# A hybrid retention and sparse-attention block: the first weighing one tile later, index pairs and selection steps at other places, the first attention scores in written order

## The chip, the cores and the metric

The kernel runs on one core of a Trainium2 chip. The metric is the device time of one execution in microseconds (us). The engines that matter here are TensorE (PE, matrix products into PSUM), VectorE (DVE), ScalarE (ACT), GpSimd (POOL) and the queue that issues most transfers (SP). Each engine works through its own list of instructions in order and waits on semaphores for the others.

## The reference

One block of a model of width 1024 over 16 meta tokens and 512 real ones, in float32: a gated feed-forward part, a mixer, a second feed-forward part and a last norm. The mixer multiplies its normalised input by one wide matrix and cuts the product into the operands of two branches:

```python
proj = u @ w_in
rq, rk, rv, rg, aq, ak, av, iq, ik, iw, g_ret, g_att = jnp.split(proj, offs, axis=-1)
# retention: 4 heads, keys of 256, values of 512, decay by distance; then a norm per head
yr = (jax.nn.silu(rg) * retention(rope(rq), rope(rk) * RET_DK**-0.5, rv)) @ w_ret_out
# sparse attention: 8 heads of 128; index scores choose the 128 keys of each query
score = einsum('bqh,bqhs->bqs', wi, relu(einsum('bqhd,bsd->bqhs', qi, ki))) * idx_scale
_, sel = lax.top_k(score, k_top)          # among admissible keys; meta keys always count
p = softmax(scores of the selected and the meta keys)
ya = (p @ v) @ w_att_out
merged = sigmoid(g_ret) * yr + sigmoid(g_att) * ya
return merged @ w_mix_out
```

## The kernel before

Every float32 product is made of three: each operand is split into a high part (a copy on ACT, `split` and `in_two`, L282 or L117) and a low part (the difference on DVE, L283 or L118), and PE adds high x high, high x low and low x high in PSUM (`mm3`, L157). A weight tile is fetched into `raw` (two buffers), split into `whi` and `wlo` (three buffers each), and used for one output tile of 128 rows; the 1024 of the inner dimension are eight steps k of three matmuls. `between` lets a projection do other work ahead of a chosen k: an entry `(4, pair)` runs `pair` ahead of k = 4.

PSUM has a ring of four one-bank tiles (`sm_tile`) and one of two two-bank tiles (`mm_tile`) in the mixer. A new tile takes the place of the fourth (second) last one and so waits for the last reader of that.

The order on PE is written by hand everywhere. In the retention part the orders on ACT and DVE are too: a list of steps, one for each weight tile, is walked by `steps_through`, which fetches and splits two tiles ahead and calls each step's matmuls and what stands behind them. For each retention head h the list has `queries_keys(h)` (two tiles of rq, two of rk), `gates_of(h)` (four tiles of rg) and `outputs(h - 1)` (four steps of two psro tiles, each added into `accr` by DVE, L1691, and behind the last the five psst tiles of the decayed score matrix of the next head, L1439 to L1443). While the projections of head h run, head h - 1 is finished: `weigh(p, c)` multiplies values by the score matrix into pspv (13 matmuls, L1460 and L1461), takes the product with the gate (`to`, L1471) and the square; `norm_sums` and `norm_all` sum the squares over all columns on PE (psn) with a diagonal matrix that `norm_diag` splits in between.

The index branch runs beside it. Its queries and keys are rotated and split (`index_queries`, `index_keys`), and `pair` takes one step of `index_steps`: two index heads for one block of 128 queries, six matmuls into two pssc tiles (L1250), a relu on ACT (L1253) and a weighted sum on DVE. There are twelve such steps; the first also transposes the index weights (psw, L1239). `pick` takes one step of `select_steps`: the next eight largest of a row and their replacement by a marker (L1267 and L1268), sixteen times for each of three blocks of 512, 384 and 256 columns; after a block's last pick, `bias` (L1270) is written. What is left of it after the last output is done beside the start of the attention.

The attention part multiplies, for each of eight heads, queries and keys into psS and psS3 (`scores`, L1864), adds the bias and takes the row maximum on DVE (L1867, L1869), the exponential on ACT (L1870) and the division on DVE (L1872, L1873); then come the projections of the next head's q and k (psaq, psak), the transposition of the probabilities (`transpose_p`, psPT, L1880) with their split, one projection of a gate (`wide_gate`), and the product with the values (psao, again `weighted`, L1460 and L1461). In this part only PE's order is written; the other engines' is made by the scheduler, except for a short stretch at the start, which stands under `manual_schedule(engines=BUSY)` and ends with the gates 4 and 5 (`gate_acc`, on POOL, L1320).

Of the kernel before, what the change touches and what calls it, by code (L numbers as in the profile page):

```python
# [18 lines left out]
P = 128  # L19
# [3 lines left out]
NM = 16  # L23
# [58 lines left out]
def kernel(ctx: ExitStack, tc: tile.TileContext, x, meta, g1, wg1, wu1, wd1, gm,  # L82
# [1247 lines left out]
    if True:  # L1330
# [207 lines left out]
        def pick(n):  # L1538

            for _ in range(n):  # L1540
                next(picks["steps"], None)
# [23 lines left out]
        def gates_of(h):  # L1565

            p = h - 1

            def behind_0(ps):
                silu(h, ps)  # L1570
                if h:
                    low = norm_diag(p)
                    if h > 1:
                        pick(1)
                    low()

            def behind_1(ps):
                silu(h, ps)
                if h == 0:
                    decayed(0)  # L1580
                    index_queries(0)
                else:
                    two_normed_parts(p, 0)

            def behind_2(ps):
                silu(h, ps)
                if h == 0:
                    index_queries(1)
                    index_queries(2)
                else:  # L1590
                    two_normed_parts(p, 2)

            def behind_3(ps):
                silu(h, ps)
                if h == 0:
                    index_queries(3)
                    values_in(0)
                    picks["pairs"] = index_steps()
                    picks["steps"] = select_steps()
                elif h == 1:  # L1600
                    for _ in picks["pairs"]:
                        pass
                else:
                    if h == RH - 1:
                        weigh(h, 0)
                    pick(3)

            sums, spread = (6, lambda: norm_sums(p)), (4, lambda: norm_all(p))
            inside = [()] * 4
            if h == 1:  # L1610
                inside = [((1, pair), (4, pair), sums), ((1, pair), spread, (6, pair)), ((1, pair), (4, pair), (6, pair)),
                          ((1, pair), (3, pair), (6, pair))]
            elif h:
                some_picks = (3, lambda: pick(1))
                inside = [(sums,), (spread,), (some_picks,), (some_picks,)]
            runs = [proj("psrg", REAL, i, b) for i, b in zip(inside, (behind_0, behind_1, behind_2, behind_3))]
            if h == 0:
                run0 = runs[0]

                def first(w, lower):  # L1620
                    bring_index()
                    run0(w, lower)

                runs[0] = first
            return steps_of(tiles(("rg", h), w_in, OFF_RG + h * DV, 4), runs)

        def queries_keys(h):

            pss, p = {}, h - 1
            ropes = heads[h]["ropes"] = {}  # L1630

            def q0(ps):
                pss["qa"] = ps
                if h == 1:
                    index_keys(0)
                    index_keys(1)
                weigh(p, 0)
                if h == 1:
                    index_keys(2)

            def q1(ps):
                pss["qb"] = ps
                ropes["q"] = rope_pieces(pss["qa"], ps, cos[:, REAL], sin[:, REAL], S, ret_q)
                some(ropes["q"], 5)
                weigh(p, 1)

            def k0(ps):
                pss["ka"] = ps
                some(ropes["q"], 1)
                weigh(p, 2)  # L1650
                some(ropes["q"], 1)

            def k1(ps):
                ropes["k"] = rope_pieces(pss["ka"], ps, cos, sin, T, ret_k)
                weigh(p, 3)

            inside = ((3, pair), (6, pair)) if h == 1 else ()
            return (steps_of(tiles(("rq", h), w_in, OFF_RQ + h * DK, 2), [proj("psrq", REAL, (), q0), proj("psrq", REAL, (), q1)])
                    + steps_of(tiles(("rk", h), w_in, OFF_RK + h * DK, 2), [proj("psrk", None, (), k0), proj("psrk", None, inside, k1)]))

        def outputs(h, beside):

# [36 lines left out]
        def beside_outputs(h):  # L1699
            def beside(i):  # L1700
                if i < 3:
                    some(heads[h + 1]["ropes"]["k"], (3, 3, 1)[i])
                pick(2 if h == 0 and i == 2 else 1)
            return beside

        last_gates, first_kq = [], []
# [17 lines left out]

        def last_2(ps):
            first_kq.append(ps)
            low = norm_diag(p)
            pick(1)
            low()

        def last_3(ps):
            first_kq.append(ps)
# [77 lines left out]
    with pool("ao") as ao:  # L1810
        vo = [ao.tile([P, AH, S], F32R, tag=f"vo{i}", name="vo") for i in range(2)]
        ao_parts = [(vo[0][:, c, :], vo[1][:, c, :]) for c in range(AH)]
        with pool("at") as at:
# [11 lines left out]
            cq, ck = (Cols(w_in, o_ + P, AH - 1, step=1) for o_ in (OFF_AQ, OFF_AK))  # L1825
            scale = DH**-0.5

            def proj_q():
                w = cq.next()
                ps = sm_tile("psaq")  # L1830
                mm3([(ps, REAL)], w, xs, KD)
                return rope_q(ps)
# [13 lines left out]
            def rope_k(ps, eng=nc.gpsimd):  # L1846
# [2 lines left out]
                split(y, k[0], k[1])  # L1849
                return k  # L1850

            def scores(q, k):
                for j in (2, 1, 0, 3):
                    n = NM + P * (j + 1)
                    qs = slice(j * P, (j + 1) * P)
                    if j < 3:
                        ps = sm_tile("psS")
                        outs = [(ps[:, : max(n, 256)], slice(0, max(n, 256)))]
                        sv = ps[:, :n]
                    else:  # L1860
                        outs, sv = halves(mm_tile("psS3"))
                    for i, (a, b) in enumerate(((q[0], k[0]), (q[0], k[1]), (q[1], k[0]))):
                        for o_, sl in outs:
                            nc.tensor.matmul(o_, a[:, qs], b[:, sl], start=i == 0, stop=i == 2)  # L1864
                    s = tmp()
                    m = at.tile([P, 4], F32, tag="stat", name="stat", bufs=8)
                    nc.vector.tensor_tensor_reduce(s[:, :n], sv, bias[j], 1.0, MARK, ALU.add,  # L1867
                                                   ALU.max, m[:, 0:1])
                    nc.vector.tensor_scalar(m[:, 1:2], m[:, 0:1], -scale, None, ALU.mult)  # L1869
                    nc.scalar.activation(prob[j][:, :n], s[:, :n], AF.Exp, bias=m[:, 1:2], scale=scale,  # L1870
                                         accum_out=m[:, 2:3])
                    nc.vector.reciprocal(m[:, 3:4], m[:, 2:3])  # L1872
                    nc.vector.tensor_scalar(prob[j][:, :n], prob[j][:, :n], m[:, 3:4], None, ALU.mult)  # L1873

            def transpose_p():
                parts = []
                for kb in range(4):
                    ps = sm_tile("psPT")
                    for j in range(max(kb - 1, 0), 4):
                        nc.tensor.transpose(ps[:, j * P : (j + 1) * P], prob[j][:, kb * P : (kb + 1) * P], ident)  # L1880
                    if kb == 3:
                        nc.tensor.transpose(ps[:NM, 0:P], prob[3][:, 4 * P : T], ident)
                    n = S - KQ[kb]
                    ph = at.tile([P, wide(n)], F32R, tag=f"pth{kb}", name="pth")[:, :n]
                    pl = at.tile([P, wide(n)], F32R, tag=f"ptl{kb}", name="ptl")[:, :n]
                    split(ps[:, KQ[kb] :], ph, pl)
                    parts.append((ph, pl))
                split_rows(ps[:NM, P - NM : P], tp["p"][:, :NM], "hlh")
                return parts

            def weigh_v(h, parts, v):
# [12 lines left out]
            with tc.manual_schedule(engines=BUSY):  # L1904
                w = gr.next()
                k, q = rope_k(first_k, nc.vector), rope_q(first_q, nc.vector)
                t, t5 = (at.tile([P, S], F32, tag="gate", name="gate", bufs=2) for _ in range(2))
                nc.scalar.activation(t, first_gate, AF.Sigmoid)
                gate_acc(4, t)
                ps = mm_tile("psgate")[:, :S]  # L1910
                mm3([(ps, REAL)], w, xs, KD)
                nc.scalar.activation(t5, ps, AF.Sigmoid)
                gate_acc(5, t5)
            for h in range(AH):
                more = h + 1 < AH
                scores(q, k)
                if h == 0:
                    vs = split_values(raw, [v[:, :4, :] for v in vo])
                    raw = fetch_values(5, vraw())
                if more:  # L1920
                    q, k = proj_q(), proj_k()
                else:
                    wide_gate()
                    wide_gate()
# [291 lines left out]
```

## Time and profile before

| | |
|---|---|
| median of 3 runs | 1543.66 us (1541.44 to 1543.89) |
| profiled execution | 1541.07 us, span 1539.3 us |
| PE busy | 1518.3 us, 99% of the span |
| DVE busy | 1092.5 us, 71% |
| ACT busy | 727.2 us, 47% |
| POOL busy | 105.7 us, 7% |
| granted clock of PE, mean | 0.997 |

The profile shows one execution. Rows of a timeline give the start on the axis of the span, the duration, the engine, the line, the operation, output <- inputs, shapes and, in brackets, how long the engine had been idle and what ended that. Buffer numbers are left out of the names, so all tiles of one name are alike.

### The profile page before, as it was taken

What the parts mean: (1) busy time and instruction counts of PE and PEld (TensorE: products, weight loads), DVE (VectorE), ACT (ScalarE), POOL (GpSimd) and SP (SyncE); (2) the same over time, 40 slices, a digit from 0 to 9 for tenths busy, and PEclk for the clock granted to TensorE, in tenths of its full rate; (3) what the DMA queues carried; (4) which work ended last, traced back from release to release, by engine and by line L of the source; (5) the groups of instructions that cost most, each with busy time, mean ns of one, the idle gap of its engine ahead of it and who ended that gap; (6) DMA issues with size and microseconds to landing.
All of it is one profiled execution on the core that took longest, in us unless ns stands there. A gap on an engine that the chain in (4) does not pass through costs nothing.

```text
span 1539.3 us, 23919 instructions
## 1 busy us (share of the span) xinstructions
PE 1518.3 (99%) x9779; PEld 1368.7 (89%) x9779; DVE 1092.5 (71%) x1672; ACT 727.2 (47%) x1138; POOL 105.7 (7%) x133
## 2 busy tenths in 40 slices
PE   9999999999999999999999999999999999999997
PEld 8999999999888887688888878998888899899996
DVE  4998585776877757676958797666455788586675
ACT  5655353554354444443333346667335356254453
POOL 1000000002111120000000122111002000000000
PEclk9999999999999999999999999999999999999999
DMA  5132333226453462232313242223343223333232
GB/s 167 60 125 90 111 102 103 98 97 218 165 197 135 141 194 91 85 127 78 117 61 99 94 126 74 83 81 116 125 149 103 97 78 101 110 103 117 83 119 87
DMA packets 150701, 173.48 MB, mean 113 GB/s; under 512 B 4928, under 2 KB 122200, under 8 KB 149952
## 3 DMA queue, kind: packets, MB, share of 16 engines
q1 hardware_dynamic: 141952, 151.58, 30.4%
q0 software_dynamic: 3808, 11.38, 1.9%
q10 hardware_dynamic: 4832, 9.00, 1.7%
q8 instruction: 76, 1.25, 0.3%
q14 instruction: 33, 0.27, 0.0%
HBM read 155.94 MB, written 16.01 MB: 112 GB/s over the span
## 4 chain that ended last, share of the span: by engine, by line
PE 85%; issue 10%; DVE 2%; ACT 1%; POOL 1%; DMA 1%; SPq 0%; ACTq 0%; POOLq 0%; DVEq 0%
PE psqX L157 14%; PE psd L157 8%; PE psd L2070 7%; PE psqY L157 7%; PE psvX L1118 4%; PE psro L157 4%; PE psqZ L157 3%; PE psak L157 3%; PE psu L157 3%; PE psga L157 3%; PE psmo L157 3%; PE psat L157 3%; PE psaq L157 3%; PE psg L157 2%; PE psgate L157 2%
## 5 line engine op out<-in xcount | busy, mean ns | idle before, releaser
L283 DVE TENSOR_TENSOR wlo<-raw,whi 128x1024 fp32r<-128x1024 f32 (+2 forms) x184 | 198.9, 1084 | 49.1 <-ACT whi L282 49.0
L282 ACT ACTIVATE whi<-raw 128x1024 fp32r<-128x1024 f32 (+2 forms) x184 | 169.8, 924 | 124.3 <-PE psd L157 37.3
L157 PE MATMUL psqX<-tl,whi 128*128 128x264 f32 (+1 forms) x432 | 122.3, 283 | 0.0
L157 PE MATMUL psqX<-th,whi 128*128 128x264 f32 (+1 forms) x432 | 122.3, 283 | 0.0
L157 PE MATMUL psqX<-th,wlo 128*128 128x264 f32 (+1 forms) x432 | 122.2, 283 | 0.0
L118 DVE TENSOR_TENSOR wlo<-raw,whi 128x1024 fp32r<-128x1024 f32 (+1 forms) x60 | 73.0, 1217 | 53.9 <-ACT whi L117 52.9
L282 ACT ACTIVATE whi<-wsum 128x1024 fp32r<-128x1024 f32 x72 | 76.3, 1060 | 70.7 <-PE psd L2070 22.0
L117 ACT ACTIVATE whi<-raw 128x1024 fp32r<-128x1024 f32 (+1 forms) x60 | 62.6, 1044 | 97.5 <-PE psat L157 26.6
L283 DVE TENSOR_TENSOR wlo<-wsum,whi 128x1024 fp32r<-128x1024 f32 x72 | 87.9, 1221 | 12.5 <-ACT whi L282 12.5
L157 PEld LDWEIGHTS psqX<-th,whi 128*128 128x128 f32 x432 | 82.1, 190 | 0.1
L157 PEld LDWEIGHTS psqX<-th,wlo 128*128 128x128 f32 x432 | 82.0, 190 | 0.0
L157 PEld LDWEIGHTS psqX<-tl,whi 128*128 128x128 f32 x432 | 82.0, 190 | 0.0
L157 PE MATMUL psro<-vo,whi 128*128 128x512 f32 x256 | 80.3, 394 | 0.5 <-DVE vo L283 0.5
L157 PE MATMUL psd<-hl,whi 128*128 128x264 f32 x352 | 71.3, 284 | 0.0
L157 PE MATMUL psd<-hh,wlo 128*128 128x264 f32 x352 | 70.7, 283 | 0.0
L157 PE MATMUL psd<-hh,whi 128*128 128x264 f32 x352 | 70.7, 282 | 0.0
L2070 PE MATMUL psd<-whi,hh 128*128 128x512 f32 x176 | 68.5, 389 | 0.0
L2070 PE MATMUL psd<-wlo,hh 128*128 128x512 f32 x176 | 68.5, 389 | 0.0
L2070 PE MATMUL psd<-whi,hl 128*128 128x512 f32 x176 | 68.5, 389 | 0.0
L157 PEld LDWEIGHTS psro<-vo,whi 128*128 128x128 f32 x256 | 48.1, 188 | 11.9 <-DVE vo L283 1.1
L157 PEld LDWEIGHTS psd<-hh,wlo 128*128 128x128 f32 x352 | 54.4, 188 | 0.0
L157 PEld LDWEIGHTS psd<-hh,whi 128*128 128x128 f32 x352 | 54.1, 188 | 0.0
(445 smaller groups left out, 4521.9 us busy)
## 6 DMA issues: line engine op xcount, KB each, us to landing
raw<-in_ffn_w_up_dram SPq DMA_DIRECT2D x22, 1024.0 KB, 5.0
raw<-in_ffn_w_gate_dram SPq DMA_DIRECT2D x21, 1024.0 KB, 5.0
raw<-in_w_in_dram SPq DMA_DIRECT2D x19, 1024.0 KB, 5.0
raw<-in_w_in_dram SPq DMA_DIRECT2D x31, 512.0 KB, 3.5
raw<-in_ffn_w_down_dram SPq DMA_DIRECT2D x24, 512.0 KB, 3.5
w<-in_w_in_dram SPq DMA_DIRECT2D x24, 512.0 KB, 6.3
raw<-in_ffn_w_down_dram SPq DMA_DIRECT2D x12, 768.0 KB, 4.3
raw<-in_w_ret_out_dram SPq DMA_DIRECT2D x8, 1024.0 KB, 4.8
```

Source lines behind the costliest of these rows:

```text
L117: nc.scalar.activation(hi, src, AF.Copy)
L118: eng.tensor_tensor(lo, src, hi.bitcast(F32), ALU.subtract)
L157: nc.tensor.matmul(o, a[:, k, :], b[:, sl], start=first and k == 0 and i == 0, stop=last and k == nk - 1 and i == 2, skip_group_check=onto)
L282: nc.scalar.activation(hi, src, AF.Copy)
L283: return lambda: nc.vector.tensor_tensor(lo, src, hi.bitcast(F32), ALU.subtract)
L1118: nc.tensor.matmul(d[bank_][t], a, b[:, k, :], start=not onto and j + k + m == 0, stop=j + k == 3 and m == 2, skip_group_check=onto)
L2070: nc.tensor.matmul(ps, a[:, bs], m[:, j, :], start=first and i == 0, stop=last and i == 2)
```

## The change

- For h = 1 the weighing of the first value tile, and with it all that hangs on it (13 matmuls, the product, the square), comes behind the second rq tile in place of the first; the three `index_keys` come together behind the first.
- The twelve index pairs get other places: one ahead of k = 5 in the first rk tile, and others in the four rg tiles.
- `norm_diag` makes its low part at once, ahead of a pick.
- More picks stand in the tiles of h = 2 and 3 and in the last two steps of `outputs(0)` to `outputs(2)`, so that all 48 and the three bias steps are done by the last output step.
- The four scores of the first attention head are written out with the two divisions of each behind all four, under the written order on PE, ACT and DVE; the next q weight is taken ahead of them. In `transpose_p` the tail rows are split ahead of the last block.

The count of instructions is the same.

```diff
@@ gates_of(h)
             def behind_0(ps):
                 silu(h, ps)
                 if h:
-                    low = norm_diag(p)
+                    norm_diag(p)()
                     if h > 1:
                         pick(1)
-                    low()
...
             if h == 1:
-                inside = [((1, pair), (4, pair), sums), ((1, pair), spread, (6, pair)), ((1, pair), (4, pair), (6, pair)),
-                          ((1, pair), (3, pair), (6, pair))]
+                inside = [((2, pair), (4, pair), sums), ((1, pair), spread, (6, pair)), ((4, pair), (6, pair)),
+                          ((3, pair), (5, pair), (7, pair))]
             elif h:
-                some_picks = (3, lambda: pick(1))
-                inside = [(sums,), (spread,), (some_picks,), (some_picks,)]
+                one_pick = (3, lambda: pick(1))
+                inside = [(sums,), (spread, (6, lambda: pick(1))), (one_pick,), (one_pick,)]
@@ queries_keys(h)
             def q0(ps):
                 pss["qa"] = ps
                 if h == 1:
-                    index_keys(0)
-                    index_keys(1)
-                weigh(p, 0)
-                if h == 1:
-                    index_keys(2)
+                    for i in range(3):
+                        index_keys(i)
+                else:
+                    weigh(p, 0)
+                    pick(1)
 
             def q1(ps):
                 pss["qb"] = ps
                 ropes["q"] = rope_pieces(pss["qa"], ps, cos[:, REAL], sin[:, REAL], S, ret_q)
+                if h == 1:
+                    weigh(p, 0)
                 some(ropes["q"], 5)
                 weigh(p, 1)
 
...
                 weigh(p, 2)
                 some(ropes["q"], 1)
+                if h > 1:
+                    pick(1)
 
             def k1(ps):
                 ropes["k"] = rope_pieces(pss["ka"], ps, cos, sin, T, ret_k)
                 weigh(p, 3)
-
-            inside = ((3, pair), (6, pair)) if h == 1 else ()
+                if h > 1:
+                    pick(1)
+
+            inside = [((5, pair),), ((3, pair), (6, pair))] if h == 1 else [(), ()]
@@ beside_outputs(h)
-                pick(2 if h == 0 and i == 2 else 1)
+                pick(2 if i > 1 else 1)
@@ last_2(ps)
-            low = norm_diag(p)
+            norm_diag(p)()
             pick(1)
-            low()
@@ attention
-            def proj_q():
-                w = cq.next()
+            def proj_q(w=None):
+                w = w or cq.next()
...
+            def score(j, q, k):
+                n = NM + P * (j + 1)
...
+                def to_one():
+                    nc.vector.reciprocal(m[:, 3:4], m[:, 2:3])
+                    nc.vector.tensor_scalar(prob[j][:, :n], prob[j][:, :n], m[:, 3:4], None, ALU.mult)
+
+                return to_one
+
             def scores(q, k):
                 for j in (2, 1, 0, 3):
...
+                    score(j, q, k)()
...
+                    if kb == 3:
+                        split_rows(ps[:NM, P - NM : P], tp["p"][:, :NM], "hlh")
                     split(ps[:, KQ[kb] :], ph, pl)
                     parts.append((ph, pl))
-                split_rows(ps[:NM, P - NM : P], tp["p"][:, :NM], "hlh")
...
                 gate_acc(5, t5)
+                w = cq.next()
+                for to_one in [score(j, q, k) for j in (2, 1, 0, 3)]:
+                    to_one()
             for h in range(AH):
                 more = h + 1 < AH
-                scores(q, k)
-                if h == 0:
+                if h:
+                    scores(q, k)
+                else:
                     vs = split_values(raw, [v[:, :4, :] for v in vo])
                     raw = fetch_values(5, vraw())
                 if more:
-                    q, k = proj_q(), proj_k()
+                    q, k = proj_q(w if h == 0 else None), proj_k()
```

More of the change, by code (lines that the diff above doesn't have):

```diff
@@ L1655, in k1 @@
                 weigh(p, 3)
-            inside = ((3, pair), (6, pair)) if h == 1 else ()
+                if h > 1:
+                    pick(1)
+            inside = [((5, pair),), ((3, pair), (6, pair))] if h == 1 else [(), ()]
             return (steps_of(tiles(("rq", h), w_in, OFF_RQ + h * DK, 2), [proj("psrq", REAL, (), q0), proj("psrq", REAL, (), q1)])
-                    + steps_of(tiles(("rk", h), w_in, OFF_RK + h * DK, 2), [proj("psrk", None, (), k0), proj("psrk", None, inside, k1)]))
+                    + steps_of(tiles(("rk", h), w_in, OFF_RK + h * DK, 2), [proj("psrk", None, inside[0], k0), proj("psrk", None, inside[1], k1)]))
         def outputs(h, beside):
@@ L1850, in rope_k @@
                 return k
+            def score(j, q, k):
+                n = NM + P * (j + 1)
+                qs = slice(j * P, (j + 1) * P)
+                if j < 3:
+                    ps = sm_tile("psS")
+                    outs = [(ps[:, : max(n, 256)], slice(0, max(n, 256)))]
+                    sv = ps[:, :n]
+                else:
+                    outs, sv = halves(mm_tile("psS3"))
+                for i, (a, b) in enumerate(((q[0], k[0]), (q[0], k[1]), (q[1], k[0]))):
+                    for o_, sl in outs:
+                        nc.tensor.matmul(o_, a[:, qs], b[:, sl], start=i == 0, stop=i == 2)
+                s = tmp()
+                m = at.tile([P, 4], F32, tag="stat", name="stat", bufs=8)
+                nc.vector.tensor_tensor_reduce(s[:, :n], sv, bias[j], 1.0, MARK, ALU.add,
+                                               ALU.max, m[:, 0:1])
+                nc.vector.tensor_scalar(m[:, 1:2], m[:, 0:1], -scale, None, ALU.mult)
+                nc.scalar.activation(prob[j][:, :n], s[:, :n], AF.Exp, bias=m[:, 1:2], scale=scale,
+                                     accum_out=m[:, 2:3])
+                def to_one():
+                    nc.vector.reciprocal(m[:, 3:4], m[:, 2:3])
+                    nc.vector.tensor_scalar(prob[j][:, :n], prob[j][:, :n], m[:, 3:4], None, ALU.mult)
+                return to_one
@@ L1852, in scores @@
             def scores(q, k):
                 for j in (2, 1, 0, 3):
[L1854 to L1871, printed above, removed]
@@ L1872, in scores @@
-                    nc.vector.reciprocal(m[:, 3:4], m[:, 2:3])
-                    nc.vector.tensor_scalar(prob[j][:, :n], prob[j][:, :n], m[:, 3:4], None, ALU.mult)
+                    score(j, q, k)()
             def transpose_p():
@@ L1913 @@
                 gate_acc(5, t5)
+                w = cq.next()
+                for to_one in [score(j, q, k) for j in (2, 1, 0, 3)]:
+                    to_one()
             for h in range(AH):
                 more = h + 1 < AH
-                scores(q, k)
-                if h == 0:
+                if h:
+                    scores(q, k)
+                else:
                     vs = split_values(raw, [v[:, :4, :] for v in vo])
```

## The prediction, made before the change was run

> **What bounds the kernel now.** I read the table of engines first, then the list of everything that TensorE (PE) waited for in the whole run.
>
> ```profile
> PE 1518.3 (99%) x9779; PEld 1368.7 (89%) x9779; DVE 1092.5 (71%) x1672; ACT 727.2 (47%) x1138; POOL 105.7 (7%) x133
> PE pspv L1460 <- ACT vo L282: 2.9, 1, 2.9
> PE psS L1864 <- ACT aq L117: 2.0, 1, 2.0
> PE psS L1864 <- DVE aq L118: 1.9, 1, 1.9
> PE pssc L1250 <- ACT tmp L1253: 1.7, 2, 1.1
> ...
> PE psn L1506 <- DVE tmp L283: 1.1, 2, 0.6
> PE psao L1461 <- issue: 0.9, 1, 0.9
> PE psro L157 <- DVE vo L283: 0.5, 2, 0.2
> ```
>
> The first row gives busy us, share and instruction count; the others what PE waited for: us in total, times, longest. PE is busy 99% and the change neither adds nor removes a matmul, so all it can win is idle time of PE. The waits that it touches sum to 2.9 + 2.0 + 1.9 + 1.7 + 1.1 + 0.9 = 10.5 us, plus matmuls that run slowly after such a wait. Everything else it does is move VectorE (DVE) work under PE's matmuls or out from under them. Times below are on the axis of this execution, 1541.07 us (its span of 1539.3 and 1.8 around it); the median of the runs is 1543.66, so I add 2.6 at the end. A measurement of this kernel can tell about 0.2%, 3.1 us, from no change.
>
> **First weighing one tile later (h = 1).** The first pspv waits for the highs of the values. The timeline there (start, duration, and in brackets the idle time before it and what ended it), and PE in the stretches of the first and the second pspv (length, busy us, granted clock, DMA share, GB/s):
>
> ```profile
> 590.02 0.50 PE L1460 MATMUL pspv<-ph,vo 128*128 128x512 f32 x1 [2.85 <-ACT vo L282]
> 590.02:592.40 2.38, 2.38 (x14) 1.00 0.83 289
> 597.97:599.98 2.01, 2.01 (x15) 1.00 0.00 0
> 586.36 1.23 DVE L283 TENSOR_TENSOR wlo<-raw,whi 128x1024 fp32r<-128x1024 f32 x1 [2.50 <-ACT whi L282]
> ...
> 590.00 2.50 DVE L283 TENSOR_TENSOR vo<-vraw,vo 128x512 fp32r<-128x512 f32 x4 [0.74 <-ACT vo L282]
> ...
> 596.35 1.41 DVE L1379 TENSOR_TENSOR ikl<-tmp,ikh 64x512 fp32r<-64x512 f32 x2
> ...
> 602.25 0.68 DVE L1402 TENSOR_TENSOR tmp<-psrq,sin 128x512 f32<-128x512 f32 x1
> 610.18 0.35 PE L1239 MATMUL psw<-ident,iw 8*128 8x8 f32 x3
> 610.46 0.50 PE L1250 MATMUL pssc<-ikh,iqh 64*128 64x512 f32 x2
> ```
>
> After the change the second rq tile starts at 587.0 in place of that wait. Its third matmul needs the weight lows that end at 587.59, so 0.2 is lost at once; the projection takes 5.6, the value parts are long done at 592.5, and both weighings and the first rk tile follow without a wait. That is 2.85 - 0.2 won, and 0.4 more because the waiting pspv took 2.38 for the matmuls that the next one does in 2.01, at a granted clock of 1.00 in both: about 3.0. [...]
>
> Then it is given back. A pair of index scores and the small transposes psw now stand inside the first rk tile, at k = 5, about 3.65 after that tile's start at 596.6, so at 600.3. They take PSUM tiles of a ring of four, whose last users are the first pspv (its square on ACT, ready about 600.5) and the two psrq tiles, read last by the fourth and fifth rope piece. DVE's queue there is unchanged but that one product `to` (0.68) goes behind the rk weight lows: index-key lows end at 597.76, weight lows 599.3, `to` 599.9, then five rope pieces at a pitch of 0.6, the last ending at about 603.0 (before: 602.25 + 0.68 = 602.9). Without a wait the second score matmul would start at 600.9, so PE stands 2.1 there. What is queued behind it is the rest of the rk tile; nobody else is held. So: 3.0 - 2.1 = 0.9 won. The bounds: nothing lost, if those tiles come free earlier than I read, and 3.0, if the rope pieces slip by another weight's lows.
>
> **Index pairs at other places.** There are twelve pairs before and after. The two waits of pssc (1.7 in all; they are at k = 1 of the last two rg tiles, where a pair follows the previous one too closely) lose their cause: no pair stands at k = 1 there now. -1.7; the other positions are at least two k steps (1.4 us of matmuls) apart, as the present (3, 6) without wait. Bounds 0 and -1.7.
>
> The first two parts together: -2.6, between -4.7 and 0.
>
> **Norm lows at once.** In h = 2 and 3 PE's psn matmul waits 0.57 twice for the low of the diagonal, which stands behind a pick:
>
> ```profile
> 718.10 0.69 DVE L1267 MAX8 top<-score 128x8 f32<-128x512 f32 x1
> ...
> 719.49 0.68 DVE L283 TENSOR_TENSOR tmp<-tmp 128x512 fp32r<-128x512 f32 x1
> ```
>
> A pick is MAX8, a load and a replacement on DVE, 1.39 from the first row's start to the second's. With it behind, the low is 1.4 earlier, or as soon as ACT's high is there, and 1.4 covers 0.57: -1.1. The pick delays the next weight lows no more than before, the sum of the two being the same.
>
> **Picks by the last output.** Thirteen picks that now lie behind the last output move ahead of it: eight into the rq, rk and rg tiles of h = 2 and 3, one, two and two into the outputs of h = 0, 1, 2. What room DVE has where they go (the stretches are outputs(0), the projections of h = 2, outputs(1), those of h = 3, outputs(2); after the length come busy us of PE, PEld, DVE, ACT, POOL, then the granted clock, DMA share, GB/s):
>
> ```profile
> 653.00:681.00 28.00, 28.00 (x136) 23.43 (x135) 22.16 (x38) 12.42 (x21) 0.00 (x0) 1.00 0.35 114
> 681.00:734.00 53.00, 52.42 (x296) 46.04 (x295) 32.29 (x48) 18.42 (x26) 3.51 (x4) 1.00 0.26 89
> 734.00:762.00 28.00, 28.00 (x136) 23.44 (x135) 27.43 (x50) 7.82 (x12) 0.00 (x0) 1.00 0.35 114
> 762.00:812.00 50.00, 49.20 (x280) 42.95 (x278) 29.62 (x44) 17.77 (x26) 3.46 (x4) 1.00 0.25 79
> 812.00:839.00 27.00, 27.00 (x130) 22.66 (x131) 23.30 (x43) 8.07 (x13) 0.00 (x0) 1.00 0.27 88
> 757.03 1.28 DVE L1691 TENSOR_TENSOR accr<-psro,accr 128x512 f32<-128x512 f32 x2
> 756.18 4.25 PE L1439 MATMUL psst<-rqk 128*128 128x512 f32 x30
> ```
>
> In the projections DVE idles 20 of 50 us, so their eight picks (1.4 at most each) are covered; I put 0.2 for one that stands just ahead of value lows for which PE already waits 0.2. In outputs(1) and (2) DVE has nothing free at the end. Two picks and a step of bias lengthen its queue ahead of the last accr sums by 1.9 and 1.1 (some picks there become narrower, which is deducted). The third psst tile takes the PSUM tile that the seventh accr frees, at 757.03 + 0.68 = 757.7, wanted by PE at about 758.8: 1.1 of slack. So 1.9 - 1.1 = 0.8 of wait there, and by the same reckoning 1.1 in outputs(2), whose slack is next to none: +1.9. Bounds 0 and 4, the four picks in full. The value lows behind are pushed back too, but have 1.3 us until they are read. outputs(0) has room for its one: DVE is busy 22.16 of 28.
>
> **First attention scores.** Thirteen picks and the bias are still to do here, and two chains wait among them in DVE's queue: the q parts for psS and the probabilities pj for psPT.
>
> ```profile
> 909.95 0.63 PE L1864 MATMUL psS<-ak,aq 128*128 128x400 f32 x2 [1.96 <-ACT aq L117]
> 912.46 2.79 PE L1864 MATMUL psS<-ak,aq 128*128 128x400 f32 x13 [1.89 <-DVE aq L118]
> 907.83:928.62 20.79, 16.95 (x102) 15.11 (x102) 19.75 (x51) 12.08 (x20) 4.20 (x3) 0.92 0.42 127
> 959.88:974.52 14.64, 14.64 (x101) 13.64 (x102) 8.49 (x27) 9.19 (x18) 2.60 (x2) 1.00 0.26 73
> 928.62:937.39 8.77, 7.90 (x40) 6.57 (x38) 8.48 (x12) 5.95 (x12) 2.15 (x2) 1.00 0.21 60
> 974.52:982.07 7.55, 7.55 (x40) 6.46 (x38) 5.75 (x10) 5.38 (x11) 1.34 (x1) 1.00 0.26 74
> 910.94 1.47 DVE L118 TENSOR_TENSOR aq<-tmp,aq 128x512 fp32r<-128x512 f32 x1
> 912.67 1.96 DVE L118 TENSOR_TENSOR wlo<-raw,whi 128x1024 fp32r<-128x1024 f32 x1
> 910.60 2.95 POOL L1320 TENSOR_TENSOR accr<-accr,gate 128x512 f32<-128x512 f32 x2 [10.79 <-ACT gate L1908]
> ```
>
> The first two stretches are the same matmuls, from the first psS to the next gate, in head 0 and in an undisturbed head: 20.79 against 14.64; the other two those from there to the next psS. So 6.15 is the most to be won there, clock included (0.92 against 1.00). DVE is busy 19.75 of 20.79 in head 0, 8.49 of 14.64 in the other. Without the picks the rope of q on DVE starts as soon as its tables land and its lows end at about 908, so psS starts at 907.8 unhindered and ends 2.3 later, at 910.1. Now the psaq tile is early: its weight highs wait on ACT for the gate's sigmoid and end at 909.6, its lows run 909.6 to 911.6 (1.96, as the row shows beside POOL's product), and its third matmul wants them at 910.6: 1.0 lost. psaq ends at 916.6, psak at 922.4. The last pj, with ACT doing table load, exponentials and the swaps of the rope in the written order, I reckon at 922.9, so 0.5 lost; psPT ends at 924.3 against 928.62: -4.3. The tail rows of p are split before the last 400 columns now, so psao's last matmul doesn't wait: 0.87, and 1.2 in all by the same comparison with a later head (8.77 against 7.55). Sum -5.5, between -2.5 and -6.6. In the later heads that edit costs nothing, as the step it delays (lows of the last block) is read last but one in psao, and 2 us are free there.
>
> About POOL: the lows ran at 910.94 and 912.67 inside its two products and took 0.8 longer each. [...]
>
> **Sum.** -2.6 - 1.1 + 1.9 + 0.2 - 5.5 = -7.1: 1541.07 - 7.1 = 1534.0, on the median's scale 1536.6.
>
> **Rivals.**
> 1. The attention chain stays late by another way, gain 2 in place of 5.5. ACT's highs of psak's weights stand ahead of the remaining exponentials in the written order, and wait for a fetch that is queued behind a transfer of 1 MB; or POOL's two products (2.95) hold the psaq lows until they end, at about 911.6, which makes the lows end at 912.8 and costs psaq 1.2 more. For: psaq and psak start 2 to 5 us earlier, their fetches do not. Against: 19.75 of 20.79 busy on DVE, most of what was late there was picks. -2.6 - 1.1 + 2.1 - 2 = -3.6: 1540.1. Chance 0.15.
> 2. No change: the waits only change their name. The wait in the rk tile eats the weighing's 3.0 in full, pssc waits as long as before at its new places, outputs(1) and (2) cost 3, attention gives 2.5: -1.1 + 3 - 2.5 = -0.6, 1543.1. For: PE's order is fixed, each gain just brings PE to the next late operand. Chance 0.12.
> 3. Slower: DVE becomes the bound from 681 to 897. Thirteen picks at 384 of 512 wide, 1.39 x 0.75 = 1.05 each, are 13.7 us; if DVE's idle time there is all dependence (it waits for PE and ACT, then has to run at once), each pick delays an accr, a low or a rope piece which PE awaits. Decided where the picks stand: as soon as more than half of their time reaches PE. In full: 13.7 - 2.6 - 1.1 - 5.5 = +4.5, 1548.2. For: 27.43 of 28 busy in outputs(1). Against: 41 of 103 us idle in the two stretches of projections, and only five of thirteen picks stand in outputs. Chance 0.12.
>
> **How the numbers follow.** My forecast has 0.61. Range: its best ends give -4.7 - 1.1 - 6.6 = -12.4 (1531.3), rival 2 reaches 1543.1; I give 1531.5 to 1543.5, which leaves out rival 3 and some tail. Faster by over 0.2%: the forecast and nearly all of rival 1, 0.75; within: rival 2 and a little, 0.13; slower 0.12.
>
> **What would show it.** Right: in the list of PE's waits no pspv, psS or psn row; a new pssc row of about 2 us in the first rk tile; psst rows of about 1 us in outputs(1) and (2); psS following the gate without a gap; the stretch from the first psS to the next gate about 16.5. Wrong: psaq or psPT waits of over 2 us, psro rows of several us from DVE, or a psw row above 3.

## The result

The changed kernel took 1537.72 us (median of 6 runs, 1536.11 to 1539.27) against 1542.77 of the kernel before (6 runs, 1541.44 to 1543.96): ratio 0.9965, interval 0.9955 to 0.9976, so 5.1 us faster. Forecast were 1536.6 and 7.1. The profiled execution of the changed kernel has a span of 1534.3 against 1539.3.

What PE waited for in the changed kernel, whole run (us in total, times, longest):

```profile
PE psst L1439 <- DVE accr L1696: 2.6, 2, 1.4
PE pssc L1250 <- DVE tmp L1402: 1.5, 1, 1.5
PE psg L606 <- DVE idle L574: 1.5, 1, 1.5
PE psaq L157 <- DVE wlo L118: 1.2, 1, 1.2
PE psPT L1891 <- DVE pj L1878: 1.0, 2, 0.5
PE psro L157 <- DVE vo L283: 0.4, 2, 0.2
PE psga L157 <- DVE stat L1872: 0.3, 1, 0.3
```

The rows of pspv, psS, psn and psao are gone, as forecast. In their place stand psst, pssc, psaq and psPT: 6.3 us of the 10.5 came back under other names. By stretches of PE's timeline, each from the start of one group of matmuls to the start of the next (us):

| stretch | before | after | change | forecast |
|---|---|---|---|---|
| up to the first rq tile of h = 2 | 679.23 | 676.20 | -3.0 | -2.6 |
| to the first psro of outputs(1) | 54.96 | 54.39 | -0.6 | -0.6 |
| to the first rq tile of h = 3 | 26.10 | 27.63 | +1.5 | +0.8 |
| to the first psro of outputs(2) | 49.54 | 48.92 | -0.6 | -0.4 |
| to the last rg tile | 26.68 | 28.37 | +1.7 | +1.1 |
| to the gate tile behind outputs(3) | 60.42 | 60.23 | -0.2 | 0 |
| to the gate tile of head 0 | 31.69 | 29.12 | -2.6 | -4.3 |
| to the first psS of head 1 | 8.77 | 7.55 | -1.2 | -1.2 |
| sum | | | -5.0 | -7.1 (-7.2 as rounded here) |

Everything behind that is as long as before (601.9 in both).

### The profile page after: what moved, and what is told of

It is laid out like the page before. It is cut to its first block, busy times and chain, and to the rows that moved or that the text cites. A ratio compares the mean times of both kernels' runs of the same rounds, so it can differ in the third digit from the quotient of the medians.

```text
span 1534.3 us, 23916 instructions
## 1 busy us (share of the span) xinstructions
PE 1517.3 (99%) x9779; PEld 1367.3 (89%) x9779; DVE 1091.4 (71%) x1672; ACT 727.2 (47%) x1138; POOL 104.7 (7%) x133
```

## The experiments

Most kernels ran once, with a profile, and are read from the stretches of their timelines. Single spans differ by 2 to 3 us for two reasons beside the edits: up to 1.2 us arise ahead of 566 us, where all these kernels are alike, and most of the rest is a slow clock that the last section shows. So where the start of a tile is compared between two runs, it is counted from the first psst matmul of each (566.52 in the changed kernel, 566.53 in the one before).

**The first term alone.** The kernel before with only the weighing later:

```diff
@@ q0, h == 1 (kernel before)
-                    index_keys(0)
-                    index_keys(1)
-                weigh(p, 0)
-                if h == 1:
-                    index_keys(2)
+                    for i in range(3):
+                        index_keys(i)
+                else:
+                    weigh(p, 0)
@@ q1
+                if h == 1:
+                    weigh(p, 0)
                 some(ropes["q"], 5)
```

> The kernel before with the first weighing one tile later and nothing else. The prediction's first term by itself: 2.85 - 0.2 of wait and 0.4 of slow matmuls, 3.0 won; the first rq tile of h = 2 starts 3.0 earlier than in the kernel before (679.2), psw and the first pair in the second rk tile wait for nothing, the two later pssc waits stay. Rival: a new wait elsewhere takes half of it, as the changed kernel's pair did.

Measured: the first rq tile of h = 2 starts 3.1 earlier than before (at 676.36, with the first psst at 566.81), one run, 1539.43 us. The pspv wait is gone and no other row of the list is new. The term holds. It is as much as the changed kernel wins up to there (3.0): the pairs' new places brought nothing on balance, two waits less against one new wait.

**The pair in the first rk tile.** The timeline of PE and DVE in the changed kernel:

```profile
600.57 0.35 PE L1239 MATMUL psw<-ident,iw 8*128 8x8 f32 x3
602.41 1.10 PE L1250 MATMUL pssc<-ikh,iqh 64*128 64x512 f32 x2 [1.50 <-DVE tmp L1402]
...
601.67 0.68 DVE L1402 TENSOR_TENSOR tmp<-psrq,cos 128x512 f32<-128x512 f32 x1
602.27 0.68 DVE L1402 TENSOR_TENSOR tmp<-psrq,sin 128x512 f32<-128x512 f32 x1
```

The first score matmul starts as the fourth rope piece ends (602.35), the second as the fifth does (602.95): the row shows 1.50 for the first, and the 1.10 of the two together hides 0.6 more. It is the 2.1 of the forecast, and each of the times is met to about 0.1. Taking the pair out:

```diff
-            inside = [((5, pair),), ((3, pair), (6, pair))] if h == 1 else [(), ()]
+            inside = [(), ((3, pair), (6, pair))] if h == 1 else [(), ()]
@@ third rg tile
-((4, pair), (6, pair)),
+((2, pair), (4, pair), (6, pair)),
```

> The changed kernel with the pair (and psw) of the first rk tile taken out; the twelfth pair goes ahead of k = 2 of the third rg tile. Theory 1: that pair's wait for the rope pieces costs what the trace of the changed kernel shows from 600.9 to 603.0, 2.1 us; then the pssc wait of 1.5 is gone, the rk tile runs without a gap, and the first rq tile of h = 2 starts 2.1 earlier (676.2 to 674.1), the span 2.1 shorter. Rival: the wait only moves to psw and the pair in the second rk tile or into the third rg tile, and the first rq tile of h = 2 starts less than 0.7 earlier.

Measured: 1.1 earlier, between the two (675.54, with the first psst at 566.93; on the bare axis it is 0.7). The 2.1 went; a new wait of 0.7 for ACT's relu came in the third rg tile, and with what it slows the pair there takes 1.91 in place of 0.80:

```profile
PE pssc L1250 <- ACT tmp L1253: 0.7, 1, 0.7
```

**The picks in the outputs.** Rows of outputs(1) in the changed kernel's timeline, PE and DVE:

```profile
752.58 2.65 PE L1439 MATMUL psst<-rqk 128*128 128x512 f32 x12
756.45 1.86 PE L1439 MATMUL psst<-rqk 128*128 128x272 f32 x18 [1.22 <-DVE accr L1696]
...
753.33 0.56 DVE L1267 MAX8 top<-score 128x8 f32<-128x384 f32 x1
...
754.58 0.56 DVE L1267 MAX8 top<-score 128x8 f32<-128x384 f32 x1
...
755.71 1.28 DVE L1696 TENSOR_TENSOR accr<-psro,accr 128x512 f32<-128x512 f32 x2
```

The third psst tile starts as the first of the two accr sums ends, behind two picks. All that DVE waited for in the changed kernel from 716 to 757:

```profile
DVE tmp L283 <- ACT tmp L282: 0.7, 1, 0.7
```

From the diagonal of the norm to here DVE has no wait for PE in this list (which leaves out waits under 0.15). It runs at its own pace, so what PE gains within that stretch (0.6 at psn) PE should give back at its end. In outputs(2) the same list has one long entry more, 3.3 for weight highs of ACT, which there wait 3.0 for their fetch; none is for PE either. Two edits, alone and together:

```diff
@@ one pick in each step of the outputs
-                pick(2 if i > 1 else 1)
+                pick(2 if h == 0 and i == 2 else 1)
@@ last_0, last_1: five picks more
+            pick(3)
             weigh(p, 1)
...
-            pick(2)
+            pick(4)
@@ behind_0: the low behind the pick
-                    norm_diag(p)()
+                    low = norm_diag(p)
                     if h > 1:
                         pick(1)
+                    low()
```

> The changed kernel with the outputs' picks as before the change (one in each step, two in one step of the first head); the five picks go behind the last two gate tiles of the stage, where DVE idles. Theory 1: the second picks alone make DVE late for the third psst tile, so both psst waits (1.2 and 1.4, 3.3 us with the slowed matmuls) go and nothing comes in their place: span 3.3 shorter. Rival: DVE is late there for another reason (three picks that stand ahead of the first step), and a wait of 0.5 or more stays in each; gain 1.5 to 2.3.

> The changed kernel with the low of the diagonal behind the pick again, for h = 2 and 3. Theory 1: DVE has no gap from there to the end of the outputs that follow, so what PE gains at psn it loses at psst; then psn waits 0.6 twice again, each psst wait becomes 0.6 shorter, and the span stays within 0.3. Rival, the prediction's own sum: the edits add up, the span is 1.1 to 1.2 longer and the psst waits are as they were.

> Both of the two edits before together: one pick in each step of the outputs, and the low behind the pick. Theory 1: without the psst waits nothing takes up the psn waits of 0.6 each, so it is 1.2 longer than with one pick alone. Rival: the psn waits are hidden whatever the picks, and it is as long as with one pick alone.

Measured, one pick: the stretches with the psst tiles are as long as in the kernel before, 3.2 less than in the changed kernel. No psst wait is left, so the second picks were the cause. But something does come in their place: the moved picks delay the last norm and the values behind it, and 2.0 is lost again (62.19 against 60.23 from the last rg tile to the gate tile behind outputs(3)). The new waits:

```profile
PE psn L1506 <- ACT tmp L282: 0.6, 1, 0.6
...
PE psro L157 <- ACT vo L282: 0.4, 1, 0.4
...
PE psn L1506 <- DVE tmp L283: 0.2, 1, 0.2
```

The low behind the pick, with two picks in the outputs. PE's waits from 700 to 850:

```profile
PE psst L1439 <- DVE accr L1697: 1.3, 2, 0.7
PE psn L1506 <- DVE tmp L283: 0.9, 2, 0.6
PE psro L157 <- DVE vo L283: 0.2, 1, 0.2
```

psst lost 1.3 of its 2.6, psn has 0.9 again, and from the first psn of h = 2 to that of h = 3 it takes 82.06 against 82.03 in the changed kernel: nothing changed. The edits don't add up. With one pick in each step, the low behind the pick costs 0.6 in h = 2 and 0.3 in h = 3, 0.9 in all: without a wait at the end of the stretch, the gain at psn stays. The theory stands, if a little less than the 1.2 expected; the sum of the prediction, which adds the two edits up, falls.

**The first attention head.** The order as before, picks early:

```diff
                 gate_acc(5, t5)
-                w = cq.next()
-                for to_one in [score(j, q, k) for j in (2, 1, 0, 3)]:
-                    to_one()
...
-                if h:
-                    scores(q, k)
-                else:
+                scores(q, k)
+                if h == 0:
```

> The changed kernel with the first attention head as before: its scores outside the written order, each division behind its own score; all picks are still done before. Theory 1: the picks in DVE's queue were what made q late, so psS still follows the gate without a gap, and from the first psS to the next psS head 0 stays within 1 us of the changed kernel's 25.6. Rival: the written order carries the gain, and psaq or psPT wait 2 us or more again.

PE's waits in it that the changed kernel doesn't have:

```profile
PE psS L1867 <- ACT aq L117: 1.5, 1, 1.5
...
PE psS L1867 <- DVE aq L118: 0.7, 1, 0.7
```

Both theories missed, though the number of the first came (24.8 from psS to psS, against 25.6). psS waits again, 2.2, but psaq and psPT no longer do. From the gate tile behind outputs(3) to that of head 0 it is 29.8, against 29.1 (changed) and 31.7 (before). So the picks carry most of the 2.6 (1.9), and the written order mainly moves the wait from psS to psaq and psPT. The 0.7 that is left goes with the clock. All three profiled executions with psS waits (this one, the kernel before, and the first term alone) have a slow clock behind them: 0.81 and 0.84 of full from 910 to 920 in the kernel before, 0.66 from 910 to 915 in the first term alone and here, which is 1.7 us lost, an estimate from 0.34 of 5 us. Without that, this order would be about 1 us shorter than the written one.

The tail rows behind the last block again:

```diff
-                    if kb == 3:
-                        split_rows(ps[:NM, P - NM : P], tp["p"][:, :NM], "hlh")
                     split(ps[:, KQ[kb] :], ph, pl)
                     parts.append((ph, pl))
+                split_rows(ps[:NM, P - NM : P], tp["p"][:, :NM], "hlh")
```

> The changed kernel with the tail rows of p split behind the last block again. Theory 1: the last matmul of head 0's psao waits about 0.9 as before the change, the span is 1.2 longer, the later heads are as they were. Rival: psao starts 4 us earlier on this axis but DVE has no picks any more, the tail rows are ready anyway, and nothing changes (within 0.2).

```profile
934.21 0.17 PE L1461 MATMUL psao<-ptail,vtail 80*128 80x16 f32 x1
930.90 0.16 DVE L1303 TENSOR_TENSOR ptail<-psPT,ptail 16x16 fp32r<-16x16 f32 x1 [0.49 <-ACT ptail L1301]
```

Nothing changed (7.58 against 7.55 from gate to psS): the tail is ready 3.1 ahead of its matmul in the old order and 4.0 in the new one. In the kernel before, DVE works without a gap from 930 to 937 and ends the tail at 937.19, ahead of its matmul at 937.29: what made it late there was DVE's backlog.

**What psaq waits for.** POOL, DVE and ACT in the changed kernel:

```profile
907.46 2.54 POOL L1320 TENSOR_TENSOR accr<-accr,gate 128x512 f32<-128x512 f32 x2 [8.86 <-ACT gate L1920]
908.85 2.23 DVE L118 TENSOR_TENSOR wlo<-raw,whi 128x1024 fp32r<-128x1024 f32 x1 [1.37 <-ACT whi L117]
911.14 0.50 PE L157 MATMUL psaq<-xh,wlo 128*128 128x512 f32 x1 [1.22 <-DVE wlo L118]
...
915.97 1.06 ACT L117 ACTIVATE whi<-raw 128x1024 fp32r<-128x1024 f32 x1 [0.98 <-DMA raw<-in_w_in_dram]
```

The lows end at 911.08, 1.08 after POOL's second product does (910.00); they take 1.22 elsewhere. So DVE seems to stand until POOL is through, about 1.0 of psaq's 1.2. Two tries to part them:

```diff
@@ first: POOL's products issued behind the scores
-                gate_acc(4, t)
...
-                gate_acc(5, t5)
...
+            gate_acc(4, t)
+            gate_acc(5, t5)
@@ second: the psaq weights ahead of the sigmoids
                 k, q = rope_k(first_k, nc.vector), rope_q(first_q, nc.vector)
+                wq = cq.next()
...
-                w = cq.next()
```

> The changed kernel with POOL's two products of accr with the gates 4 and 5 issued behind the first scores in place of ahead of them. Theory 1: POOL's products hold the lows of the psaq weights (2.23 in place of 1.22) and with them psaq's third matmul (1.22), the fetch of the next weights and so the exponential and psPT (1.0); then the psaq wait falls to 0.2 or less, the psPT waits to half, and the next gate comes 1.5 to 2.5 earlier. Rival: the lows are late because ACT makes the highs late, and the psaq wait stays above 0.8.

> The changed kernel with the psaq weights of head 1 taken, and so split, ahead of the two sigmoids of the gates 4 and 5 (moving POOL's products behind the scores in the program had changed nothing: POOL ran them at the same place). Theory 1: the lows then run on DVE before POOL's products start, in 1.2 in place of 2.2, and end ahead of psaq's third matmul: no psaq wait (1.2 before), the fetch of the psak weights for the head after starts 2 us earlier, and the psPT waits (1.0) go too; the stretch from the end of outputs to the next gate is 1.5 to 2.3 shorter than the changed kernel's 29.1. Rival: POOL and DVE disturb each other at another place, or the highs delay the q parts, and less than 0.6 is won.

The first changed nothing (psaq 1.2, lows 2.24): POOL has nothing else in its queue (it idles 8.86 us ahead of the products in the changed kernel and 8.64 here) and starts when the first sigmoid is there, at both places in the program. It tested nothing. The second, POOL and DVE:

```profile
910.36 1.22 DVE L118 TENSOR_TENSOR wlo<-raw,whi 128x1024 fp32r<-128x1024 f32 x1 [0.26 <-ACT whi L117]
...
911.03 3.94 POOL L1320 TENSOR_TENSOR accr<-accr,gate 128x512 f32<-128x512 f32 x2 [9.70 <-ACT gate L1921]
```

Now DVE comes first and takes 1.22, and POOL's two products take 3.94. psaq and psPT wait for nothing, and the stretch is 26.1 against 29.1: 3.0 won, more than was expected. The edit puts the lows ahead of POOL and starts them earlier against psaq at the same time, so it doesn't say how much of the 3.0 is the wait beside POOL and how much the earlier start.

**Together.**

> The three together: no pair in the first rk tile, one pick in each step of the outputs, POOL's products behind the scores. Theory 1: the parts add, 2.1 + 3.3 + 2 = 7.4 us shorter than the changed kernel, 12 shorter than the kernel before, ratio 0.992. Rival: each gain is taken up by the next late operand, and it is less than 4 us shorter than the changed kernel.

Measured: 1534.09 (5 runs, 1533.09 to 1535.40), ratio 0.9943 (0.9930 to 0.9957), 3.6 less than the changed kernel: the rival, by the waits that the moved pair and picks made, and with one of its three edits without effect. With better places:

```diff
@@ pairs: none in the first rk tile; third and fourth rg tile
+((3, pair), (6, pair)), ((1, pair), (3, pair), (5, pair), (7, pair))
@@ picks: outputs as in the kernel before; behind both weighings of last_0, and in the last outputs
+            pick(3)
-        more += outputs(p, lambda i: pick(2))
+        more += outputs(p, lambda i: pick(2 + (i > 1)))
@@ attention: the psaq weights ahead of the sigmoids
```

> The changed kernel with what the runs so far point to: the pair of the first rk tile goes to k = 1 of the last rg tile, with the pairs of the third at 3 and 6; the extra picks go out of the outputs, three behind the second weighing of the last gate tile and one more in each of the last two steps of the last outputs; the psaq weights ahead of the sigmoids. Theory 1: no pssc wait and no slow clock behind it (2.1 and about 1.6 on the median), no psst waits (3.3), no psaq and psPT wait (1.5 to 2.3): 8 shorter than the changed kernel, near 1530. Rival: the moved picks and pairs make new waits as in the two tries before, and it stays within 1.5 of 1534.1, that of the first combination.

Measured: 1531.44 (5 runs, 1529.68 to 1532.47), ratio 0.9927 (0.9914 to 0.9941), 6.3 less than the changed kernel: between the two. The waits of psst, psaq, psPT and psn are gone; the last rg tile has a pssc wait of 1.5 at k = 1, and a slow clock behind it (0.66 from 645 to 650). Last, the pairs of both tiles at k = 3, 5 and 7:

> As the last combination, with the pairs of the third rg tile at k = 3, 5, 7 and of the fourth at 3, 5, 7, none at k = 1. Theory 1: a pair waits where it meets ACT at the start of a tile, busy with the gate and the normed parts; away from there no pssc wait is left, and with it goes the slow clock behind it: 1.5 of wait and about 1.7 of clock, 3 shorter than the last combination on the profile, 1 to 3 on the median (1528.5 to 1530.5). Rival: two k steps are too close for pairs of 384 columns wherever they stand, a pssc wait of 0.7 or more stays in the third rg tile, and the median is within 1 of 1531.4.

```profile
PE psg L606 <- DVE idle L574: 1.5, 1, 1.5
PE psro L157 <- DVE vo L283: 0.5, 2, 0.2
PE pssc L1250 <- ACT tmp L1253: 0.4, 1, 0.4
PE psga L157 <- DVE stat L1873: 0.3, 1, 0.3
PE psrq L157 <- DVE wlo L283: 0.2, 1, 0.2
```

Measured: 1529.59 (5 runs, 1529.09 to 1531.37), ratio 0.9916 (0.9902 to 0.9929) to the kernel before, about 13 us. That is within what was expected; a pssc wait of 0.4 is left where none was to be, without a slow clock behind it.

## Why the prediction was right, and where its steps were off

The sign, the range and most places were right: which waits go, which four come, and that the sum is a gain. The size is 2.1 short on this execution (-5.0 for -7.1): 1.3 at the picks and 1.7 in the first attention head, against 0.8 better elsewhere.

- *First weighing* (3.0): 3.1 alone. Right to the mechanism.
- *Index pairs* (-1.7, and 2.1 at the pair in the rk tile): right in the places, and on balance close (0.1 lost, forecast 0.4), but the -1.7 was too small. It counted the two gaps alone; in the kernel before the two pairs with them take 1.87 and 2.08, where pairs of their widths take 0.80 and 0.62 without a wait, so 2.5 went. The pair in the rk tile cost 2.2. Another 0.4 went in outputs(0), whose 96 psro matmuls take 22.56 in place of 22.15; the runs don't show why. The step also left out the clock behind the wait in the rk tile, last section.
- *Norm lows at once* (-1.1): at psn 1.2 won, as costed. *Picks* (+1.9): +3.2. (The 0.2 for the value lows didn't come: psro waits 0.4, before 0.5.) The step that failed is the slack at the third psst tile. It was read off the kernel before, with PE's start as it was, while PE now came 0.6 earlier to a stretch in which DVE doesn't wait for PE. 0.8 + 0.6 and 1.1 + 0.6 give the 1.5 and 1.7 measured. The two edits together cost 2.0 where the sum had 0.8.
- *First scores* (-5.5): -3.8. The psaq wait (1.0 forecast, 1.2 measured) and a late psPT (0.5, 1.0) were foreseen in kind, but mis-sized with their consequences: the psaq tile takes 6.97 from its start to psak's, 5.48 in head 1. Weight highs on ACT waited 0.98 for a fetch ahead of an exponential, as in the first rival, though those of a later tile than psak; and the psaq lows ended 1.08 after POOL's products (2.23 in place of 1.22), also as there, which the sum already had in its 1.96 for the lows. So that rival's places were right, its price (3.5 less) too large. Taking the psaq weights earlier removed both waits of PE.
- The tail rows: the 1.2 came, but by luck: with the old order of the split it comes as well, and so it does without the written order of the scores. What these kernels share is that the picks are done.
- The third rival had the right place (outputs, DVE full) and was too dear: DVE's late picks cost 3.2, not 13.7.

## What to carry to other kernels

A gain on the bounding engine lasted here only to the next place where a queue that doesn't wait for that engine catches it (the 0.6 of psn was gone at the third psst tile): before adding gains, look in each stretch for whether the helper engine idles waiting for the bounding one, and count the gains within such a stretch once. When work is moved out of one full stretch, put it where the helper does wait for the bounding engine, and split weights ahead of a POOL product that would run beside their lows (1.22 ahead of it here, 2.23 beside it). Work moved by program text alone didn't move on an engine whose queue was empty: POOL's products started with the first sigmoid from both places.

## What the runs showed of the hardware

**Behind the wait of 2.1 us in the first rk tile the clock was slow in seven of eight executions.** PE behind that wait, in the profiled execution of the changed kernel (length, busy us, granted clock, DMA share, GB/s):

```profile
605.00:610.00 5.00, 5.00 (x40) 1.00 0.00 0
```

And in that of the kernel with the low behind the pick, which is the same up to there:

```profile
600.00:605.00 5.00, 3.40 (x25) 0.96 0.68 209
605.00:610.00 5.00, 5.00 (x27) 0.70 0.00 1
```

Of eight executions profiled with that wait seven show the dip, with 1.6 to 3.4 us more up to outputs(0); of six without it none does there. Five of the seven lose 1.6 or 1.7, two 3.2 and 3.4. The two rows above give 1.7, an estimate from 0.04 and 0.30 of 5 us. The profiled execution of the changed kernel is the one without a dip, and its 1536.11 is the fastest of its six runs; so the dip is probably part of the median, though the other five runs have no profile that could show it. The kernel before has its own in the first attention head (0.81 and 0.84 from 910 to 920). The length of a wait alone doesn't tell: waits of 1.5 and 0.6, with a few small matmuls around them, came ahead of these dips, where 2.85 at the first pspv of the kernel before cost no clock in its one profiled execution (1.00 from 590.02 to 592.40). What sets the dip off, and why one execution of eight has none, the runs don't show.

**POOL's products and the lows on DVE ended one behind the other.** POOL's row in the kernel before (910.60, 2.95) holds two products, one of 1.26 and one of 1.73, as the list by source line shows (shortest, median and longest in ns, then the two starts):

```profile
L1320 POOL TENSOR_TENSOR accr<-accr,gate x2: 1264/1496/1727, 910.6 to 911.8; 128x512 f32<-128x512 f32 x2
```

The first ends at 911.86, and the lows of aq, begun meanwhile, 0.55 later (912.41); POOL's second ends 1.14 after aq (913.55); the weight lows, begun meanwhile, 1.08 after that. By themselves aq takes 0.69, such a product 1.28, the lows 1.22: each time the later one ends its own length, less about 0.14, after the other. So the 0.8 that each of the two lows took longer there was a wait for one product. The runs show the same: in the changed kernel the lows end 1.08 after POOL's last product (910.00); with the psaq weights ahead of the sigmoids they come first and take 1.22, while POOL's pair goes from 2.54 to 3.94 and ends 1.15 after the next lows on DVE. In the timeline such an instruction looks like a slow one: the lows of the changed kernel are shown with 2.23, from 908.85. Not every operation of DVE waits so: in the changed kernel a rope piece at 918.67 takes its 0.69 beside a product of POOL at 918.71, which takes 1.29.
